# A decoder trunk on one core: the last pair of products reordered and stored in halves, the first weights loaded in blocks of two features

## The chip, the cores and the metric

The kernel runs on one core of a Trainium2 chip. The metric is the device time of one execution in microseconds; the number given for a kernel is the median of several runs.

A core has five engines that run at the same time and wait for one another through semaphores: TensorE (PE, matrix products; its weight loads are shown as PEld), VectorE (DVE), ScalarE (ACT), GpSimd (POOL) and SyncE (SP), which here only issues transfers. ScalarE and GpSimd can issue transfers too. Matrix products are written to PSUM, eight banks of 128 x 512 numbers; everything else lies in SBUF.

## What is computed

Two layers of a transformer trunk over 512 tokens of width 1024, in float32. Each layer has four parts, each added to the running sum x:

```python
x = x + 0.5 * swiglu(rms_norm(x, ffn1_norm[l]), ffn1_w_gate[l], ffn1_w_up[l], ffn1_w_down[l])
h = rms_norm(x, mix_norm[l])
a, g, q, k, v = split(h @ w_in[l])
# conv_out: a * sigmoid(g), causal depthwise convolution of width 31, rms_norm, silu
# diff_out: differential attention of q, k, v with a relative-position bias
x = x + concat([conv_out, diff_out]) @ w_out[l]
x = x + 0.5 * swiglu(rms_norm(x, ffn2_norm[l]), ffn2_w_gate[l], ffn2_w_up[l], ffn2_w_down[l])
# swiglu(h, g, u, d) = (silu(h @ g) * (h @ u)) @ d, inner width 2816
```

The result is x after the second layer.

## The kernel before, in words

**Layout.** x lies in SBUF with its width over the partitions: `x[:, k, :]`, k = 0 to 7, is one tile of 128 features by 512 tokens. Below, "feature k" means that tile of 128 features.

**Products in three parts.** A float32 operand is split into a high part (`whi` for weights, `acth` for activations), made by a copy on ScalarE, and the rest (`wlo`, `actl`), made by a subtraction on VectorE. One product then is three matmuls (`mm3`, lines 200, 203 and 204): high x high, high weight x low activation, low weight x high activation. Weights come from HBM into a ring of five buffers `wraw`, and their parts go to rings of nine buffers each.

**The start.** A few products of a tile of ones (`WARM`, line 228) run before any data is there. Then the first four weight tiles, gate and up for two output tiles, are loaded as two halves of four features each (`half`), and each half in blocks of columns that `cuts` gives: one feature and three features for the first half, all four at once for the second. For each block SP issues the first feature of x in it (line 238), the four weight blocks (line 241), and the rest of the features (line 247). Each weight block is converted on its own (lines 242, 243). `Prep.tile` makes `acth` and `actl` of each feature (lines 309, 310). `lead_products` multiplies all eight features with the four tiles, feature by feature; then the row sums of squares (`ssum`, lines 318 to 322) are transposed on TensorE (line 268).

`started` holds the last conversion on ScalarE and on VectorE of one block. The squares of x (on ScalarE) and the small scalars of `make_scalars` (on VectorE) are put behind it in their engines' order with `behind`. Before, that block is the last one of the first half.

**The order of the work.** A planner orders each engine's instructions, by a timeline that it simulates while the kernel is built; what is ready first in that timeline can go ahead of what stands earlier in the program. Calls of `keep_in_program_order` pin the first matmul of a group to its place among the pinned ones, and `behind` puts an engine's instructions after a given one. Waits between engines follow from the data.

**The feed-forward parts.** They use seven products of half-sized blocks in place of eight (Strassen's scheme in Winograd's form). The weight sums that it needs are made by loads that add on arrival (`wsum`, issued by GpSimd, line 160) and on VectorE (lines 175, 176). For the down projection a `Pair` computes two output tiles, m and m2 = m + 4, in two PSUM banks, each cut in two halves of 256 tokens: `a`, `d` in the first, `b`, `c` in the second. Each call of `go` (line 524) is one of the seven products; here it takes four steps of three matmuls, twelve in all. In the last pair (m = 3) the order on TensorE is: `c` (`t1`, in `head`, saved to `keep` at line 531), `d` (`t4`), the last product of the pair before, `a` (`b11`, after which both halves of the bank are saved, line 557), `b` (`b21`), `c` (`b22`), `a` (`t2`, saved at line 561), and in `finish` `a` (`t3`). `a` is a running sum: each product adds to it, so a save must have read it before the next product changes it.

Tile m = 3 is finished on VectorE by lines 563 and 564, once `c` holds everything. Tile 7 is finished in `finish`: line 570 adds a saved part to `d`'s place, line 571 another to `a`, and line 572 adds -0.5 times both to x. Then `store` (line 1070) writes the tile to HBM; each of the eight tiles is stored as soon as it is done, in one transfer on SP's queue. The function `tail` calls `finish` and the last `store`.

Of the kernel before, what the change touches and what calls it, by code (L numbers as in the profile page):

```python
# [15 lines left out]
ALU = mybir.AluOpType  # L16
# [6 lines left out]
KT = DM // P  # L23
# [14 lines left out]
MASK = -1e30  # L38
RLEN = 640
STATS_AT = 5  # L40
WARM = 9
TAIL_AT = 2
HS = SEQ // 2

# [26 lines left out]
def trunk(ctx: ExitStack, tc: tile.TileContext, xt, par, lamv, relb, onehot,  # L71
          gu1, dn1, wag, wqkv, wout, gu2, dn2, out):
    nc = tc.nc
    V, S, G, T = nc.vector, nc.scalar, nc.gpsimd, nc.tensor
# [9 lines left out]
    def f32(ap):  # L84
        return ap.bitcast(F32)
# [3 lines left out]
    def bank(tag, name):  # L89
        return psum.tile([P, 512], F32, tag=tag, name=name, bufs=BANKS[tag])  # L90
# [4 lines left out]
    def ring(tag, n=512):  # L95
        dt = F32R if tag in ("whi", "wlo") else F32
        return wp.tile([P, 512], dt, tag=tag, name=tag, bufs=RING[tag])[:, :n]
# [109 lines left out]
    x = act.tile([P, KT, SEQ], F32, tag="x", name="x")  # L207
# [17 lines left out]
    warm = bank("tp", "ps_warm")  # L225
    for _ in range(WARM):
        tc.keep_in_program_order(
# [1 line left out]
        )  # L229

    lead = [[] for _ in range(4)]
    for half, cuts in enumerate(((0, 1, 4), (0, 4))):
        tiles = [(ring("wraw"), ring("whi"), ring("wlo")) for _ in lead]
        for w, (_, hi, lo) in zip(lead, tiles):
            w.append((hi, lo))
        for k, k2 in zip(cuts, cuts[1:]):
            to = slice(k * P, k2 * P)
            nc.sync.dma_start(x[:, half * 4 + k, :], xt[half * 4 + k])
            for n, (raw, hi, lo) in enumerate(tiles):
                src = slice((half * 4 + k) * P, (half * 4 + k2) * P)  # L240
                nc.sync.dma_start(raw[:, to], gu1[0, n // 2, n % 2][:, src])
                big = S.activation(hi[:, to], raw[:, to], AF.Copy)
                low = V.tensor_tensor(out=lo[:, to], in0=raw[:, to], in1=f32(hi[:, to]), op=ALU.subtract)
            if k2 == 4 and not half:
                started = big, low
            for j in range(half * 4 + k + 1, half * 4 + k2):
                nc.sync.dma_start(x[:, j, :], xt[j])
    lead = [lead[2 * m : 2 * m + 2] for m in range(2)]
# [122 lines left out]
    def pair_banks():  # L371
        tag = ("sc", "po", "mm")[next(turns) % 3]
        return [bank(tag, "ps_pair") for _ in range(2)]
# [131 lines left out]
    class Pair:  # L505
# [10 lines left out]
        def go(self, ps, weight, xt, js=None):  # L516
            at = self.hid.get(xt)
            side = 0 if ps is self.a or ps is self.d else 1
            wh, wl = weight
            for i, j in enumerate(range(self.hid.n) if js is None else js):  # L520
                f = slice(j * P, (j + 1) * P)
                xh, xl = at(j)
                for l, (s, r) in enumerate(((wh, xh), (wh, xl), (wl, xh))):
                    mm = T.matmul(ps, s[:, f], r, start=side not in self.begun, stop=False, skip_group_check=True)  # L524
                    self.begun.add(side)
                    if i == l == 0:
                        tc.keep_in_program_order(mm)
# [3 lines left out]
            self.saved = S.activation(self.keep[:, self.kc], self.c, AF.Copy)  # L531
            return self

        def body(self, w, before, more=None):
            a, b, c, d, go = self.a, self.b, self.c, self.d, self.go
            both = self.banks[0].rearrange("p (n c) -> p n c", n=2)
            if self.m == 0:
                n = self.hid.n
                most, rest = range(n - 1), range(n - 1, n)
                go(a, w["g1"], "b11")  # L540
                more(S.activation(self.keep[:, 0], a, AF.Copy))
                go(b, w["g2"], "b21", most)
                go(d, w["u2"], "t4", most)
                nxt = before()
                go(c, w["all"], "b22", most)
                go(a, w["g1u2u1"], "t2", most)
                go(b, w["g2"], "b21", rest)
                go(c, w["all"], "b22", rest)
                go(d, w["u2"], "t4", rest)
                go(a, w["g1u2u1"], "t2", rest)  # L550
                saves.append(S.activation(self.keep[:, 2:], both, AF.Copy))
            else:
                nxt = None
                go(d, w["u2"], "t4")
                before()
                go(a, w["g1"], "b11")
                S.activation(self.keep[:, :2], both, AF.Copy)
                go(b, w["g2"], "b21")
                go(c, w["all"], "b22")
                go(a, w["g1u2u1"], "t2")  # L560
                saves.append(S.activation(self.keep[:, 2], a, AF.Copy))
            two, xm = self.banks[1].rearrange("p (n c) -> p n c", n=2), x[:, self.m, :]
            V.tensor_tensor(two, two, self.keep[:, 0::2], op=ALU.add)
            V.scalar_tensor_tensor(xm, self.banks[1], 0.5, xm, op0=ALU.mult, op1=ALU.add)
            return nxt

        def finish(self, weight):
# [3 lines left out]
            V.tensor_tensor(a, a, self.keep[:, self.kd], op=ALU.add)  # L571
            V.scalar_tensor_tensor(xn, self.banks[0], -0.5, xn, op0=ALU.mult, op1=ALU.add)

    def begin(pr, loads, tail=None):
        ws = [[chunk(src) for src in pair] for pair in loads]
        ps = [pair_banks() for _ in loads]
        return [*zip(ws, ps)], first_products(pr, ws, ps, early=tail is not None, tail=tail)

    def ffn(fp, pr, gu, dn, after, begun, then, spare, aside=None):
        halves = None  # L580
        late = []
        jobs = []
# [29 lines left out]
        for fs, kind in PARTS:  # L612
            many = len(fs)
            hh, held = [], []
            if kind == "first":
                for mm, m in enumerate(fs):
# [7 lines left out]
                    else:  # L624
                        w, ps = [chunk(gu[m, 0]), chunk(gu[m, 1])], pair_banks()
# [16 lines left out]
                    if m == 1:  # L642
                        halves = Halves(fp, pr, r)
# [5 lines left out]
                w = banks = None  # L649
                for m in range(KT):  # L650
# [3 lines left out]
                    for kk in range(many):  # L654
                        b = m * many + kk
                        if b % 4 == 0:
                            w = [gather(dn, blocks[b : b + 4])]
# [11 lines left out]
            this = group(part=True)  # L669
            finish()  # L670
            pair = None
            for m in range(KT // 2):
                m2 = m + KT // 2
                if m == 0:

                    def more(saved):
                        with behind(saved, hid.last[0]):
                            this.split("all", "g1u2u1", "g1u1")

                    with behind(hid.big, hid.sum):  # L680
                        ahead[0].split("u2u1")
                    pair = Pair(hid, fp, m, m2).head(this.w["u2u1"])
                    nxt = pair.body(this.w, lambda: Pair(hid, fp, 1, 1 + KT // 2).head(ahead[0].w["u2u1"]), more)
                else:
                    this = group(after=hid.last if m == 1 else ())
                    pair = nxt if m == 1 else Pair(hid, fp, m, m2).head(this.w["u2u1"])
                    pair.body(this.w, finish)
                if kind == "last":
                    if m:
                        after(m2 - 1)  # L690
                    after(m)
                late.append(lambda pair=pair, this=this: pair.finish(this.w["g1u1"]))

        def tail():
            finish()
            after(KT - 1)

# [347 lines left out]
    pr = Prep(0, "ffn1_norm")  # L1045
# [12 lines left out]
    begun = [*zip(lead, banks)], lead_products(pr, lead, banks)  # L1058
    for l in range(DEPTH):
        nxt = {}  # L1060

        def preparing(gain, l2=l):
            def after(m):
                if m == 0:
                    nxt["p"] = Prep(l2, gain)
                nxt["p"].tile(m)
            return after

        def store(m):
            nc.sync.dma_start(out[m], x[:, m, :])  # L1070

        with tc.tile_pool(name="ffn", bufs=1) as fp:
            begun = ffn(fp, pr, gu1[l], dn1[l], preparing("mix_norm"), begun,
                        lambda tail: begin(nxt["p"], [[wag[l, c, i] for i in range(2)] for c in range(2)], tail),
                        (l == 0, 1), aside if l == 0 else None)
        mixer(l, nxt["p"], preparing("ffn2_norm"), begun)
        with tc.tile_pool(name="ffn", bufs=1) as fp:
            begun = begin(nxt["p"], [[gu2[l, m, i] for i in range(2)] for m in range(2)])
            if l + 1 < DEPTH:
                begun = ffn(fp, nxt["p"], gu2[l], dn2[l], preparing("ffn1_norm", l + 1), begun,  # L1080
                            lambda tail: begin(nxt["p"], [[gu1[l + 1, m, i] for i in range(2)] for m in range(2)], tail), (0, 1))
            else:
                ffn(fp, nxt["p"], gu2[l], dn2[l], store, begun, lambda tail: tail(), (0, 0))
        pr = nxt["p"]


# [72 lines left out]
```

## Time and profile before

| what | value |
|---|---|
| median of 3 runs | 1771.87 us (1771.71 to 1772.9) |
| the profiled execution | 1772.54 us |
| its span, first to last instruction | 1770.8 us |
| TensorE busy | 1759.9 us, 11853 matmuls |
| VectorE busy | 1470.9 us |
| ScalarE busy | 1039.5 us |
| GpSimd busy | 515.1 us |
| transferred | 257.79 MB |

The profile shows one execution. Times are counted from the span's start. A row of a group or of the order of time names the source line, the engine, the operation and the tiles as output<-inputs; what stands in square brackets behind a row is the engine's idle time before it, and what ended that. Matmuls are pipelined: the next starts before the one before has ended, so their lengths overlap, and idle time appears only where the gap is longer than that overlap. A row "x4" merges four neighbours, with the time from the first start to the last end. Rows marked SPq or ACTq are the issues of transfers; the time to landing runs from the issue until the data has arrived. The chain of waits follows the work that ended last backwards, from each instruction to what released it.

### The profile page before, as it was taken

What the parts mean: (1) busy time and instruction counts of PE and PEld (TensorE: products, weight loads), DVE (VectorE), ACT (ScalarE), POOL (GpSimd) and SP (SyncE); (2) the same over time, 40 slices, a digit from 0 to 9 for tenths busy, and PEclk for the clock granted to TensorE, in tenths of its full rate; (3) what the DMA queues carried; (4) which work ended last, traced back from release to release, by engine and by line L of the source; (5) the groups of instructions that cost most, each with busy time, mean ns of one, the idle gap of its engine ahead of it and who ended that gap; (6) DMA issues with size and microseconds to landing.
All of it is one profiled execution on the core that took longest, in us unless ns stands there. A gap on an engine that the chain in (4) does not pass through costs nothing.

```text
span 1770.8 us, 32986 instructions
## 1 busy us (share of the span) xinstructions
PE 1759.9 (99%) x11853; PEld 1621.3 (92%) x11853; DVE 1470.9 (83%) x2642; ACT 1039.5 (59%) x1951; POOL 515.1 (29%) x497
## 2 busy tenths in 40 slices
PE   9999999999999999999999999999999999999998
PEld 7799999988788899999988999999887888999998
DVE  7969888969877969889987798899698678698987
ACT  6546566755865436566644565666559554465664
POOL 1011112169970011112200121121798600111122
PEclk9999999999999999999999999999999999999999
DMA  7457677533223457687544577766231335577774
GB/s 222 135 135 184 166 197 190 135 122 96 71 78 113 123 130 178 172 198 177 143 144 108 149 176 180 194 161 177 81 113 48 101 105 134 133 184 173 194 176 126
DMA packets 165894, 257.79 MB, mean 146 GB/s; under 512 B 19191, under 2 KB 61958, under 8 KB 165728
## 3 DMA queue, kind: packets, MB, share of 16 engines
q1 hardware_dynamic: 129024, 201.38, 36.7%
q0 software_dynamic: 36416, 54.12, 19.0%
q8 instruction: 93, 1.52, 0.3%
q14 instruction: 73, 0.60, 0.1%
q10 hardware_dynamic: 288, 0.16, 0.0%
HBM read 253.48 MB, written 3.42 MB: 145 GB/s over the span
## 4 chain that ended last, share of the span: by engine, by line
PE 95%; DVE 2%; DMA 1%; POOL 1%; ACT 1%; issue 0%; SPq 0%; ACTq 0%; DVEq 0%; POOLq 0%
PE ps_pair L435 36%; PE ps_pair L524 17%; PE ps_pair L203 9%; PE ps_pair L204 9%; PE ps_pair L200 9%; PE ps_out L200 2%; PE ps_out L203 2%; PE ps_out L204 2%; PE ps_pair L815 2%; PE ps_pair L814 2%; PE ps_pair L813 2%; PE ps_sc L930 1%; PE ps_v L844 1%; PE ps_v L843 1%; PE ps_v L845 1%; POOL wlo L102 0%
## 5 line engine op out<-in xcount | busy, mean ns | idle before, releaser
L101 ACT ACTIVATE whi<-wraw 128x512 fp32r<-128x512 f32 x744 | 454.0, 628 | 421.9 <-PE ps_pair L203 174.8
L102 DVE TENSOR_TENSOR wlo<-wraw,whi 128x512 fp32r<-128x512 f32 x640 | 427.0, 685 | 116.7 <-ACT whi L101 105.2
L160 POOL DMA_DIRECT2D wsum<-in_gu x128 | 112.2, 907 | 703.7 <-DMA wsum<-in_gu 276.0
L435 PE MATMUL ps_pair<-acth,wlo 128*128 128x256 f32 x1024 | 289.8, 283 | 0.0
L435 PE MATMUL ps_pair<-actl,whi 128*128 128x256 f32 x1024 | 289.8, 283 | 0.0
L435 PE MATMUL ps_pair<-acth,whi 128*128 128x256 f32 x1024 | 289.8, 283 | 0.0
L435 PE MATMUL ps_pair<-th,whi 128*128 128x256 f32 x768 | 217.3, 283 | 0.0
L435 PE MATMUL ps_pair<-tl,whi 128*128 128x256 f32 x768 | 217.3, 283 | 0.0
L435 PE MATMUL ps_pair<-th,wlo 128*128 128x256 f32 x768 | 217.3, 283 | 0.0
L200 PE MATMUL ps_pair<-acth,whi 128*128 128x512 f32 x512 | 199.4, 394 | 0.5 <-ACT acth L309 0.4
L203 PE MATMUL ps_pair<-actl,whi 128*128 128x512 f32 x512 | 199.5, 390 | 0.3 <-DVE actl L310 0.3
L204 PE MATMUL ps_pair<-acth,wlo 128*128 128x512 f32 x512 | 199.2, 390 | 0.0
L435 PEld LDWEIGHTS ps_pair<-actl,whi 128*128 128x128 f32 x1024 | 196.6, 192 | 0.2
L435 PEld LDWEIGHTS ps_pair<-acth,whi 128*128 128x128 f32 x1024 | 196.6, 192 | 0.2
L435 PEld LDWEIGHTS ps_pair<-acth,wlo 128*128 128x128 f32 x1024 | 196.6, 192 | 0.0
L160 POOL DMA_DIRECT2D wsum<-in_dn x112 | 98.8, 1132 | 266.6 <-DMA wsum<-in_dn 45.6
L435 PEld LDWEIGHTS ps_pair<-th,whi 128*128 128x128 f32 x768 | 147.5, 192 | 0.0
L435 PEld LDWEIGHTS ps_pair<-tl,whi 128*128 128x128 f32 x768 | 147.5, 192 | 0.0
L435 PEld LDWEIGHTS ps_pair<-th,wlo 128*128 128x128 f32 x768 | 147.5, 192 | 0.0
L102 POOL TENSOR_TENSOR wlo<-wraw,whi 128x512 fp32r<-128x512 f32 x104 | 137.1, 1339 | 31.8 <-ACT whi L101 19.5
L524 PE MATMUL ps_pair<-hh,whi 128*128 128x256 f32 x512 | 144.9, 283 | 0.0
L524 PE MATMUL ps_pair<-hl,whi 128*128 128x256 f32 x512 | 144.9, 283 | 0.0
(207 smaller groups left out, 4445.2 us busy)
## 6 DMA issues: line engine op xcount, KB each, us to landing
wraw<-in_gu SPq DMA_DIRECT2D x284, 256.0 KB, 3.5
wsum<-in_gu SPq DMA_DIRECT2D x128, 256.0 KB, 3.8
wsum<-in_gu POOLq DMA_DIRECT2D x128, 256.0 KB, 4.7
wraw<-in_dn SPq DMA_DIRECT2D x68, 256.0 KB, 3.3
wraw<-in_wqkv SPq DMA_DIRECT2D x48, 256.0 KB, 2.9
wraw<-in_wout SPq DMA_DIRECT2D x48, 256.0 KB, 3.0
wraw<-in_dn SPq DMA_DIRECT2D x64, 128.0 KB, 4.2
wraw<-in_wag SPq DMA_DIRECT2D x32, 256.0 KB, 3.0
```

What stands on the lines that cost most here:

```text
L101: S.activation(hi, raw, AF.Copy)
L102: (eng or V).tensor_tensor(out=lo, in0=raw, in1=f32(hi), op=ALU.subtract)
L160: nc.gpsimd.dma_start(dst[:, to], src, accum_op=ALU.add)
L200: first = T.matmul(ps, wh, xh, start=start, stop=False)
L203: T.matmul(ps, wh, xl, start=False, stop=False)
L204: T.matmul(ps, wl, xh, start=False, stop=stop)
L435: mm = T.matmul(ps, l, r, start=first and i == j == 0, stop=False, skip_group_check=True)
L524: mm = T.matmul(ps, s[:, f], r, start=side not in self.begun, stop=False, skip_group_check=True)
L813: T.matmul(ps[n], xh[:, t], wh, start=k == 0, stop=False)
L814: T.matmul(ps[n], xh[:, t], wl, start=False, stop=False)
L815: T.matmul(ps[n], xl[:, t], wh, start=False, stop=k == KT - 1)
L843: T.matmul(ps, xh[:, t], wh, start=k == 0, stop=False)
```

## The change

Four edits.

- The products of ones (`WARM`) go from nine to eight.
- The first weights come in blocks of two features throughout: `cuts` becomes (0, 2, 4) for both halves. There are sixteen weight transfers of 128 KB in place of four of 64, four of 192 and four of 256 KB. x's features 0, 2, 4 and 6 go ahead of their block, and 1, 3, 5 and 7 behind it. `started` is set by every block, so it ends up as the last block of the second half.
- In the last pair of the last feed-forward part, `b22` (into `c`) comes after `t2` and its save in place of before them.
- The last tile of the output, tile 7, is finished in another way there: -0.5 times the two saved parts is added to x by one operation on 512 columns, ahead of the product `t3`; after `t3`, -0.5 times `a` is added to each half of 256 tokens, and each half is stored by a transfer of its own, the first issued on SP and the second on ScalarE's queue.

```diff
-WARM = 9
+WARM = 8
...
-    for half, cuts in enumerate(((0, 1, 4), (0, 4))):
+    for half, cuts in enumerate(((0, 2, 4), (0, 2, 4))):
...
-            if k2 == 4 and not half:
-                started = big, low
+            started = big, low
...
-        def body(self, w, before, more=None):
+        def body(self, w, before, more=None, last=False):
...
                 go(b, w["g2"], "b21")
-                go(c, w["all"], "b22")
+                if not last:
+                    go(c, w["all"], "b22")
                 go(a, w["g1u2u1"], "t2")
                 saves.append(S.activation(self.keep[:, 2], a, AF.Copy))
+                if last:
+                    go(c, w["all"], "b22")
...
+        def finish_halves(self, weight, store):
+            a, xs = self.a, x[:, self.m2, :].rearrange("p (n c) -> p n c", n=2)
+            V.scalar_tensor_tensor(xs, self.keep[:, 1::2], -0.5, xs, op0=ALU.mult, op1=ALU.add)
+            self.go(a, weight, "t3")
+            for n, queue in enumerate((nc.sync, nc.scalar)):
+                V.scalar_tensor_tensor(xs[:, n], a, -0.5, xs[:, n], op0=ALU.mult, op1=ALU.add)
+                store(n, xs[:, n], queue)
...
-                    pair.body(this.w, finish)
+                    pair.body(this.w, finish, last=kind == "last" and end and m == KT // 2 - 1)
...
-        def tail():
+        def tail(halves=None):
+            if halves:
+                late.clear()
+                pair.finish_halves(this.w["g1u1"], halves)
+                return
             finish()
             after(KT - 1)
...
+        def store_half(n, half, queue):
+            queue.dma_start(out[KT - 1][:, n * HS : (n + 1) * HS], half)
...
-                ffn(fp, nxt["p"], gu2[l], dn2[l], store, begun, lambda tail: tail(), (0, 0))
+                ffn(fp, nxt["p"], gu2[l], dn2[l], store, begun, lambda tail: tail(store_half), (0, 0), end=True)
```

More of the change, by code (lines that the diff above doesn't have):

```diff
@@ L577, in begin, with ffn @@
         return [*zip(ws, ps)], first_products(pr, ws, ps, early=tail is not None, tail=tail)
-    def ffn(fp, pr, gu, dn, after, begun, then, spare, aside=None):
+    def ffn(fp, pr, gu, dn, after, begun, then, spare, aside=None, end=False):
         halves = None
```

## The prediction

> **What bounds the kernel now.** I read the page first (busy time by engine), then TensorE's waits, then the matmuls at both ends in order of time, because the change touches nothing else.
>
> ```profile
> PE 1759.9 (99%) x11853; PEld 1621.3 (92%) x11853; DVE 1470.9 (83%) x2642; ACT 1039.5 (59%) x1951; POOL 515.1 (29%) x497
> ```
> ```profile
> PE ps_pair L524 <- ACT keep L557: 0.9, 2, 0.5
> ...
> PE ps_pair L524 <- ACT keep L561: 0.5, 1, 0.5
> ```
> ```profile
> 30.00:1700.00 1670.00, 1667.37 (x11209) 1535.42 (x11208) 1395.04 (x2498) 984.91 (x1848) 497.66 (x471) 1.00 0.56 144
> ```
>
> TensorE is busy for 1759.9 of 1770.8 us, so the change can win only what TensorE loses: some 11 us in all. In the 1670 us between the ends it loses 2.6 (the row of a stage: its length, then TensorE's busy time), so what is to be had lies in the first 30 us and behind the last products, where the diff works: one wait there is that on the save of line 561. Matmuls are pipelined, so the waits shown are too small; the loss is read from start to start.
>
> TensorE's first products in order of time (start, length, line, out<-in, count):
>
> ```profile
> 1.44 4.21 PE L228 MATMUL ps_warm<-ones_r 128*128 128x512 f32 x9 [1.44 <-DVE ones_r L221]
> 5.44 0.81 PE L200 MATMUL ps_pair<-acth,whi 128*128 128x512 f32 x2
> 6.10 0.63 PE L203 MATMUL ps_pair<-actl,whi 128*128 128x512 f32 x2
> ...
> 8.63 0.39 PE L203 MATMUL ps_pair<-actl,whi 128*128 128x512 f32 x1
> 9.09 0.50 PE L200 MATMUL ps_pair<-acth,whi 128*128 128x512 f32 x1
> ...
> 11.07 0.61 PE L204 MATMUL ps_pair<-acth,wlo 128*128 128x512 f32 x2
> 12.10 1.20 PE L200 MATMUL ps_pair<-acth,whi 128*128 128x512 f32 x4 [0.42 <-ACT acth L309]
> 13.58 0.50 PE L203 MATMUL ps_pair<-actl,whi 128*128 128x512 f32 x1 [0.28 <-DVE actl L310]
> ...
> 15.53 1.07 PE L200 MATMUL ps_pair<-acth,whi 128*128 128x512 f32 x4
> ...
> 29.13 0.60 PE L268 MATMUL ps_rows<-ident,ssum 128*128 128x128 f32 x4
> ```
>
> Undisturbed, four products take 1.07 us, so one follows another after (1.07 - 0.39)/3 = 0.227. The first products are 8 features x 4 tiles x 3 = 96, or 21.8 us; from 5.44 to 29.13 they take 23.7. Of the 1.9 too many, 0.2 is the first one still at half pace; the rest is three stalls, after 8.63, 11.07 and 12.10, some 1.6 with the slow restart behind each.
>
> **The change part by part: the start.** What stalled them is in ScalarE's and VectorE's rows; SP's issues, their time to landing and a piece of the chain of waits follow:
>
> ```profile
> 10.30 0.61 ACT L318 ACTIVATE ssum<-x 128x512 f32<-128x512 f32 x1
> 10.82 0.61 ACT L321 ACTIVATE sq<-x 128x512 f32<-128x512 f32 x1
> 11.35 0.71 ACT L309 ACTIVATE acth<-x,par 128x512 fp32r<-128x512 f32 x1
> ...
> 11.88 0.68 DVE L322 TENSOR_TENSOR ssum<-ssum,sq 128x512 f32<-128x512 f32 x1
> ...
> 12.78 0.75 DVE L310 SCALAR_TENSOR_TENSOR actl<-x,par,acth 128x512 fp32r<-128x512 f32 x1
> ```
> ```profile
> 3.05 0.43 SPq L238 DMA_DIRECT2D x<-in_xt  x1
> ...
> 5.70 0.90 SPq L247 DMA_DIRECT2D x<-in_xt  x2
> ...
> x<-in_xt SPq DMA_DIRECT2D x1, 256.0 KB, 3.2
> ...
> x<-in_xt SPq DMA_DIRECT2D x1, 256.0 KB, 4.8
> ...
> 5.22 4.62 DMA wraw<-in_gu
> ```
>
> Feature 2 of x, issued at 5.70, landed 4.8 later, at 10.5; ScalarE then did two squares before its `acth` at 11.35, and VectorE a sum of squares and small scalars before its `actl` at 12.78. With `started` set by the last conversion of the last block, squares and scalars queue behind all sixteen conversions and can't come before feature 2. That removes the second and third stall (0.81 - 0.23 = 0.58 and 0.67 - 0.23 = 0.45 between starts, 0.11 each for the restart). The first (0.46 - 0.23 = 0.23, and 0.11) waited for the three-feature blocks; with two features in the first block, feature 1 needs no second load.
>
> Whether loads keep up I count in bytes on SP's queue ahead of each piece (par's 159 KB included; a tile of x is 256 KB, a block of two features 128). Before, x1 landed at 3.05 + 3.2 = 6.25 after 927 KB, the last three-feature block at 9.84 after 1695, x2 at 10.5 after 1951. After, x1 is complete at 1183 KB: 6.25 + 256/768 x 3.59 = 7.4, its `acth` 0.71 later at 8.2, and TensorE ends feature 0 at 8.3. The second blocks end at 1951 KB, at 10.5, 10.9 with a conversion of some 0.4; TensorE wants feature 2 at 11.0. So it fits, by a hair: I take 1.5 of the 1.6, and 0 to 1.6 as ends. The four issues more (at 0.43) delay the next group's loads on SP from 12.3 to some 13.9; these wait for buffers and are wanted at 27, so nothing. The squares move on ScalarE from 10.3 to about 18: eight at 0.61 and their sums end by 25, where the transposes of the row sums would start at 27.4. Cover stays.
>
> One product of ones fewer: 4.21 us hold nine, so one is about 0.43. But the first real product needs its converted weights:
>
> ```profile
> 4.54 1.00 ACT L242 ACTIVATE whi<-wraw 128x128 fp32r<-128x128 f32 x4
> ...
> 5.02 0.76 PEld L200 LDWEIGHTS ps_pair<-acth,whi 128*128 128x128 f32 x2
> ...
> 1756.33 0.36 ACT L531 ACTIVATE keep<-ps_pair 128x256 f32<-128x256 f32 x1
> ```
>
> The first 128-column conversion starts at 4.54; one of 256 columns takes 0.36, so the weight load starts at 4.9 to 4.95 in place of 5.02: 0.1 gained (ends 0 and 0.43). Start: 1.6 in all. It reaches the end, since TensorE has almost no idle time until then and its weights wait for buffers that it frees itself.
>
> **The end.**
>
> ```profile
> 1759.26 0.60 ACT L557 ACTIVATE keep<-ps_pair 128x512 f32<-128x512 f32 x1 [2.57 <-PE ps_pair L524]
> ...
> 1763.26 0.28 PE L524 MATMUL ps_pair<-yh,wlo 128*128 128x256 f32 x1
> 1763.58 0.38 ACT L561 ACTIVATE keep<-ps_pair 128x256 f32<-128x256 f32 x1 [3.72 <-PE ps_pair L524]
> 1763.99 0.70 DVE L563 TENSOR_TENSOR ps_pair<-ps_pair,keep 128x512 f32<-128x512 f32 x1 [4.54 <-ACT keep L561]
> 1764.01 0.38 PE L524 MATMUL ps_pair<-yh,whi 128*128 128x256 f32 x1 [0.47 <-ACT keep L561]
> 1764.72 0.69 DVE L564 SCALAR_TENSOR_TENSOR x<-ps_pair,x 128x512 f32<-128x512 f32 x1
> ...
> 1765.42 0.28 PE L524 MATMUL ps_pair<-yh,wlo 128*128 128x256 f32 x1
> 1765.73 0.43 DVE L570 TENSOR_TENSOR ps_pair<-ps_pair,keep 128x256 f32<-128x256 f32 x1 [0.32 <-PE ps_pair L524]
> 1766.67 0.69 DVE L572 SCALAR_TENSOR_TENSOR x<-ps_pair,x 128x512 f32<-128x512 f32 x1
> ```
> ```profile
> 1765.44 2.28 SPq L1070 DMA_DIRECT2D out<-x  x2
> ...
> GB/s 0 0 0 0 0 0 0 0 137 382 423 396 341 69 0 0 0 0 0 0 0 164 369 410 396 355 55 55 0 0 0 0 0 0 0 0 0 0 0 0
> ...
> out<-x SPq DMA_DIRECT2D x2, 256.0 KB, 2.1
> ```
>
> Today the twelve `t2` products end at 1763.54, ScalarE saves them, and only then may the twelve `t3` products overwrite: the last starts at 1765.42. With the `b22` products between, the save (0.38) lies under 12 x 0.12 = 1.44 us of products, `t3` follows without a gap, and its last starts at 1763.26 + 1.44 = 1764.70, 0.72 earlier, ending at 1764.98. VectorE now starts line 563 at about 1763.57 and line 564 at 1764.30, through at 1764.99. The new product of `keep` with -0.5 (512 columns, 0.69) needs saves that exist at 1759.9, or 1762.5 if the strided read is held to wait for the save of `t2`; VectorE is idle there for 4.54 us, so I price it at nothing (0.6 if it is ordered behind line 564). The halves take 0.43 each in place of 0.43 + 0.43 + 0.69: the first from 1765.01 to 1765.44, the second, overlapping, to 1765.79, where line 572 ended at 1767.36.
>
> Stores: tile 3's issue moves from 1765.44 to 1765.03; the halves are issued at about 1765.47 on SP and 1765.82 on ScalarE's idle queue. In the GB/s row (0.15 us a slice, from 1765) 256 KB begin 0.85 after the issue and flow for 0.85; landing comes at 2.1. Three stores together are 512 KB, from 1765.88 to 1767.6, and land at 1768.0; today the last is issued at 1767.39 and lands at 1769.49. Gain 1.5. Were the queues to have separate engines, the last half would land about 1.65 after its issue, at 1767.5 (gain 2.0); with the 0.6 above, 0.9. I take 1.5, nearest to the rate of the row, which is near 400 GB/s for a store alone.
> The Trainium skill ("DMA: Bandwidth & Descriptors", Issuing engines are not separate DMA queues) says that issuing from several engines saves the sequencer's time only. By that rule the sum keeps 1.5; without it 2.0. No run yet shows two store queues at once.
>
> **Sum.** 1772.54 (the profiled execution; its span is 1770.8) - 1.6 - 1.5 = 1769.4. The median of the three runs, 1771.87, lies 0.67 lower, so 1768.8.
>
> **The rivals.** (1) More than the sum: a stall elsewhere goes with the shift (line 557 has 0.9) or the second half finds free engines (0.5) or the weights are ready for the whole 0.43: about 0.9 more, 1767.9. For it: thin waits; against: nothing in the diff aims there.
> (2) The start brings nothing: the larger blocks come late and each feature waits again. For it: margins of 0.1 above; against: the early loads, 64 KB per 0.43 us of issue, leave the engines room, and the squares are gone in any case. 1768.8 + 1.6 = 1770.4.
> (3) TensorE's clock rises later. The products of ones start (4.21 - 0.63) / 8 = 0.45 apart and the first two real ones 0.42, from 6.10 on it is 0.23: full pace came 4.5 us after the first start at 1.44. If the gap of some 0.1 before the real products makes that count begin anew at 5.35, it comes at 9.85; about 3.95 us at half pace lose half, 2.0: 1770.8. Against it: the gap is shorter than a product.
> The Trainium skill ("TensorE: Matmul & The Clock Gate", Part 1) says that the gate looks at free-running windows of about 3.4 us of activity and doesn't count products. By it eight products or nine matter only through that gap, and one window later would cost 1.7, an estimate from the page's figure. The trace shows one rise and not where a window begins, so it bears out neither.
> (4) Slower than before. The order of ScalarE, VectorE, SP and POOL is written by a planner from its own clock, which the start shifts; one accumulating weight load moved behind others in its queue is late by a transfer. In the chain one takes this long:
>
> ```profile
> 1742.83 6.04 DMA wsum<-in_dn
> ```
>
> TensorE lost 0.5 on line 557 just behind that transfer, so there is no slack there and another 6.0 would come whole: 1768.8 + 6.0 = 1774.8. It decides from 3.1 us on. Against it: the 2.6 us lost between the ends so far, and an order that follows from buffers which TensorE frees.
>
> **How the numbers follow.** What a measurement of this kernel can tell from no change is about 0.2%, 3.5 us: below 1768.3 is faster, above 1775.4 slower. Forecast 0.55 (a third of it below 1768.3, own range 1767.8 to 1769.8); (1) 0.18; (2) and (3) 0.15; (4) 0.12, two thirds of it above 1775.4. Faster 0.18 + 0.18 = 0.36, slower 0.08, same 0.56. The range runs from the best ends of the start (2.0) and of the end (2.0) with 0.7 of the waits between, 1768.8 - 0.4 - 0.5 - 0.7 = 1767.2, to rival (3) with the 0.6 of the end lost as well and 0.2 over, 1771.6.
>
> **What would show it.** Starts of the first 96 products: 22 us from first to the transposes, none over 0.3 apart, squares after 17 us. At the end no gap before `t3`, line 563 beginning with it, two 256-column products on `out`'s last tile, last landing about 3.1 us earlier. Wrong if the stalls return at features 1 to 3, if products run at half pace past 6.5 us, if `keep` x -0.5 stands behind line 564, or if a new wait appears between 30 and 1750 us.

## The result, and the profile after

The median fell from 1772.16 to 1768.97 us (22 runs of each), 3.2 us; the ratio is 0.9984, with a 95% interval of 0.9977 to 0.999, or 1.8 to 4.1 us less. The forecast was 1768.8.

The profiled execution is not a typical one: at 1772.28 us it is the slowest of the 22. TensorE's waits in it and two pieces of the chain of waits say why:

```profile
PE ps_pair L523 <- ACT keep L556: 2.3, 2, 2.1
PE ps_pair L523 <- ACT keep L530: 1.6, 1, 1.6
```
```profile
1093.55 6.10 DMA wsum<-in_gu
```
```profile
1742.31 8.22 DMA wsum<-in_dn
```

ScalarE converts weights and saves parts in one queue. Where a weight load that adds on arrival is late, the save behind its conversion is late (lines 530 and 556 after are 531 and 557 before), and TensorE waits. The piece at 1742 took 6.04 before and 8.22 here. The same kernel in another execution (1769.81 us, span 1768.0; all its waits of TensorE) lost next to nothing there:

```profile
PE ps_warm L228 <- DVE ones_r L221: 1.4, 1, 1.4
PE ps_o L974 <- ACT at L967: 1.1, 2, 0.5
PE ps_sc L944 <- DVE e L958: 0.8, 2, 0.4
PE ps_pair L523 <- ACT keep L556: 0.4, 2, 0.2
PE ps_pair L200 <- DVE gs L642: 0.3, 1, 0.3
```

Neither list has the old waits on `acth`, `actl` and on the save of line 561; a wait on `gs` (line 642) is new. By stages, from the starts of TensorE's matmuls in the order of time (us):

| | before | after, first profile | after, second profile |
|---|---|---|---|
| first real product | 5.44 | 5.02 | 5.02 |
| clock at full pace from | 5.8 | 5.0 | 7.4 |
| first product of the first seven-product stage | 107.97 | 106.43 | 107.42 |
| first product of the last four pairs' run | 1723.79 | 1723.81 | 1723.20 |
| last product of all | 1765.42 | 1766.36 | 1763.87 |
| from there to the end of the span | 5.35 | 4.14 | 4.15 |

The start after, first profile, in the order of time:

```profile
1.44 3.74 PE L228 MATMUL ps_warm<-ones_r 128*128 128x512 f32 x8 [1.44 <-DVE ones_r L221]
5.02 0.40 PE L200 MATMUL ps_pair<-acth,whi 128*128 128x512 f32 x1
5.35 0.50 PE L203 MATMUL ps_pair<-actl,whi 128*128 128x512 f32 x1
...
7.99 1.07 PE L200 MATMUL ps_pair<-acth,whi 128*128 128x512 f32 x4
...
10.71 0.62 PE L200 MATMUL ps_pair<-acth,whi 128*128 128x512 f32 x2
...
28.39 0.60 PE L267 MATMUL ps_rows<-ident,ssum 128*128 128x128 f32 x4
...
38.67 0.40 PE L204 MATMUL ps_pair<-acth,wlo 128*128 128x512 f32 x1
39.32 0.50 PE L200 MATMUL ps_pair<-acth,whi 128*128 128x512 f32 x1 [0.25 <-DVE gs L642]
```

The first real product follows the last product of ones with no gap, and from 5.35 to 38.67 no stall stands between two products. (The row sums' transposes come at 28.39, not 27.4, because the planner put six products of the third tile ahead of them.) At 39.32 TensorE is held up: 0.65 from start to start in place of 0.23.

The end, second profile: ScalarE's save and TensorE around `t3`'s first product (1762.55), VectorE's operations, SP's and ScalarE's issues, the stores' time to landing:

```profile
1761.31 0.38 ACT L561 ACTIVATE keep<-ps_pair 128x256 f32<-128x256 f32 x1 [2.28 <-PE ps_pair L523]
```
```profile
1762.43 0.28 PE L523 MATMUL ps_pair<-hh,wlo 128*128 128x256 f32 x1
1762.55 0.28 PE L523 MATMUL ps_pair<-yh,whi 128*128 128x256 f32 x1
```
```profile
1762.83 0.70 DVE L565 TENSOR_TENSOR ps_pair<-ps_pair,keep 128x512 f32<-128x512 f32 x1 [3.07 <-PE ps_pair L523]
1763.56 0.69 DVE L566 SCALAR_TENSOR_TENSOR x<-ps_pair,x 128x512 f32<-128x512 f32 x1
1764.19 0.76 DVE L581 SCALAR_TENSOR_TENSOR x<-ps_pair,x 128x256 f32<-128x256 f32 x2
```
```profile
1764.28 0.33 SPq L1084 DMA_DIRECT2D out<-x  x1
1764.72 0.37 SPq L1087 DMA_DIRECT2D out<-x  x1
```
```profile
1764.98 0.35 ACTq L1087 DMA_DIRECT2D out<-x  x1
```
```profile
out<-x SPq DMA_DIRECT2D x1, 256.0 KB, 2.0
out<-x SPq DMA_DIRECT2D x1, 128.0 KB, 2.0
out<-x ACTq DMA_DIRECT2D x1, 128.0 KB, 2.1
```

The save now lies under products, `t3` goes on at the usual 0.12, and the second half is issued 1.10 us after the last product's start, where the whole tile was issued 1.97 after it before. The halves are 128 KB and land as long after their issue, 2.0 to 2.1, as 256 KB do.

### The profile page after: what moved, and what is told of

The parts are those of the page before. It is cut to its first block, busy times and chain, and to the rows that moved or that the text cites. A ratio compares the mean times of both kernels' runs of the same rounds, so it can differ in the third digit from the quotient of the medians.

```text
span 1770.5 us, 33000 instructions
## 1 busy us (share of the span) xinstructions
PE 1758.8 (99%) x11852; PEld 1620.9 (92%) x11852; DVE 1470.9 (83%) x2646; ACT 1037.4 (59%) x1955; POOL 516.1 (29%) x497
## 4 chain that ended last, share of the span: by engine, by line
PE 94%; DVE 2%; DMA 1%; POOL 1%; ACT 1%; issue 1%; DVEq 0%; ACTq 0%; SPq 0%; POOLq 0%
PE ps_pair L434 36%; PE ps_pair L523 16%; PE ps_pair L200 9%; PE ps_pair L203 9%; PE ps_pair L204 9%; PE ps_out L200 2%; PE ps_out L203 2%; PE ps_out L204 2%; PE ps_pair L829 2%; PE ps_pair L828 2%; PE ps_pair L827 2%; PE ps_sc L944 1%; PE ps_v L858 1%; PE ps_v L859 1%; PE ps_v L857 1%
## 5 line engine op out<-in xcount | busy, mean ns | idle before, releaser
L102 DVE TENSOR_TENSOR wlo<-wsum,whi 128x512 fp32r<-128x512 f32 x192 | 130.0, 683 | 23.7 <-ACT whi L101 23.4
```

Source lines behind the costliest of these rows:

```text
L102: (eng or V).tensor_tensor(out=lo, in0=raw, in1=f32(hi), op=ALU.subtract)
```

## The experiments

Each kernel was timed beside the kernel before on the same chip; "before" is its median there.

**The two ends apart.** Only the three edits of the start, and only those of the end:

```diff
 start_only, against the kernel before
-WARM = 9
+WARM = 8
-    for half, cuts in enumerate(((0, 1, 4), (0, 4))):
+    for half, cuts in enumerate(((0, 2, 4), (0, 2, 4))):
-            if k2 == 4 and not half:
-                started = big, low
+            started = big, low
 end_only, against the changed kernel: these lines as before
```

> The three edits of the start alone (eight products of ones, blocks of two features, squares behind the last block), the end as before. Theory (two separate gains that TensorE carries to the end): 1.6 us below the kernel before, read in the trace as the first matmul of the seven-product stage starting at 106.4 in place of 108.0 us, and no two of the first 96 products over 0.35 us apart once the clock is up; the end from the last product on takes as long as before (5.35 us from the last start of a matmul to the end of the span). Rival (start brings nothing that lasts, all is won at the end): same time as before, first seven-product matmul at 108.0 or later stages that take it back.

> The edits of the last pair and of the last store alone, the start as before. Theory: 1.5 us below the kernel before by the prediction's sum; the two profiles so far give 0.7 us between the last pair's first product and its last, and 1.2 us from there to the end of the span, 1.8 together. First seven-product matmul at 108.0 as before. Rival (the end gains only the removed wait, 0.7 us, since three stores crowd on the same engines): 0.7 below the kernel before.

Measured: start 1771.24 against 1772.62 before (0.9992, 0.9984 to 1.0001), end 1770.97 (0.9994, 0.9986 to 1.0003): 1.4 and 1.7 us, 3.0 together, about the whole change. Each interval alone just reaches 1, but the traces show each gain at its place. With the start alone the first seven-product matmul stands at 106.61 (before 107.97); with the end alone the last product's start comes 40.75 us after that of the last run of pairs (before 41.63), and the rest takes 4.72 us (before 5.35). So both gains arise, each without the other, and the rival of the end falls.

Whether the start's gain lasts to the end is less clear. In the profile with the start alone the last run of pairs begins at 1723.52, only 0.27 before the 1723.79 of before: of the lead of 1.36 TensorE lost 1.0 near 1100 us, on the save of line 530. The three profiles with the old start (before, `end_only` and `swap_only` below) have the first seven-product matmul at 107.76 in the mean and the last run of pairs at 1723.55; the five with all edits of the start and eight products of ones (both of the changed kernel, `start_only`, and `halves_sp` and `whole_store` below) have them at 106.84 and 1723.63. The lead is 0.9 in the mean and then gone: four of the five lost 1.0 to 1.6 near 1100 us. But these five executions were 1.1 us longer in the mean than their kernels' medians, and the three 0.6 shorter. That the gain lasts in a typical execution rests on the medians: 1.4 here, and 2.6 for the blocks alone below, whose interval excludes no change.

One expectation failed: with the start alone the time behind the last product fell too, from 5.35 to 5.01, although no instruction of it changed. After the last landing SP runs down a list of waits on semaphores at 0.06 each. From the one that waits for that landing on, seven are left before, three with the start alone, six with the end alone and two in the changed kernel. Of the 0.34 here, 0.24 is that list; the store itself landed 0.09 earlier.

**How many products of ones.**

```diff
-WARM = 8
+WARM = 9    (ones_nine, against the changed kernel)
+WARM = 5    (ones_five)
```

> The changed kernel with nine products of ones in place of eight. Theory (the first product waits for its weights, so the ninth product costs little): 0.1 us above the changed kernel, first real product at 5.4 us. Rival (the weights are there, the whole product of ones is on the path): 0.4 us above it. If the clock's rise depends on the count of products, it comes at the same place in both.

> The changed kernel with five products of ones in place of eight, so that TensorE is idle for about 1 us before the first real product. Theory of the prediction's third rival (an idle gap makes the clock's count begin anew): full pace comes 4.5 us after the first real product, at about 9.4 us, and the kernel is 2.0 us slower than the changed one. Rival (the gate looks at windows whose place does not depend on the kernel, and a gap of 1 us in a window may or may not count): full pace between 5 and 9 us, differing from one execution to the next, 0 to 1.7 us slower.

Measured: nine 1769.25, five 1771.38, beside 1772.62 before. Nine starts its first real product at 5.44, where eight start it at 5.02 without a gap: the weights are ready early enough, and the ninth product is wholly on the path (the rival, 0.4); in time it is 0.3 above the changed kernel's 22 runs, within noise. Five, in the order of time on TensorE:

```profile
2.46 1.48 PE L228 MATMUL ps_warm<-ones_r 128*128 128x512 f32 x3
4.94 0.80 PE L200 MATMUL ps_pair<-acth,whi 128*128 128x512 f32 x1 [1.00 <-ACT whi L242]
...
7.33 0.63 PE L200 MATMUL ps_pair<-acth,whi 128*128 128x512 f32 x1
7.75 0.63 PE L203 MATMUL ps_pair<-actl,whi 128*128 128x512 f32 x1
...
10.31 1.41 PE L200 MATMUL ps_pair<-acth,whi 128*128 128x512 f32 x4
11.56 0.39 PE L203 MATMUL ps_pair<-actl,whi 128*128 128x512 f32 x1
11.79 0.39 PE L204 MATMUL ps_pair<-acth,wlo 128*128 128x512 f32 x1
```

One microsecond of idle time, and products start 0.43 apart, half pace, until about 11.0, 6.1 us after the first real one. The kernel is 2.1 us slower than with nine, near the 2.0 of the count that begins anew; but that theory put the rise at 9.4, and it came 1.6 later. The Trainium skill ("TensorE: Matmul & The Clock Gate", Part 1) has free-running windows of some 3.4 us. With eight or nine products full pace came between 4.4 and 7.4 us in the thirteen profiles of before, after and the other experiments, a spread of 3.0, narrower than one such window, and with five at 11.0, 3.6 behind the latest of them. The traces' own rows of the granted clock agree with the page: the stretch at full clock lasts 1764.69 us in seven of the thirteen, 1761.28 in the other six and 1757.86 with five, in steps of 3.41. How much idle time in a window delays the rise stays open. One profile of the five doesn't exclude another rule: in the thirteen the rise came 3.0 to 6.0 us after TensorE's first product, and with five 6.1 us after the first product behind the gap, so a count that begins anew there would nearly fit too.

**Blocks against squares.** The kernel before with the new `cuts` alone, and with the new place of `started` alone:

```diff
 blocks_only
-    for half, cuts in enumerate(((0, 1, 4), (0, 4))):
+    for half, cuts in enumerate(((0, 2, 4), (0, 2, 4))):
 squares_late
-            if k2 == 4 and not half:
-                started = big, low
+            started = big, low
```

> The kernel before with blocks of two features alone: nine products of ones, and squares and scalars still queued behind the first half's last block. Theory A (each edit removes its own stall, as the prediction had it): only the stall that waited for the three-feature blocks goes, 0.3 us, and squares and scalars still hold up a feature: first seven-product matmul 0.3 us earlier than before. Theory B (the squares now stand ahead of feature 4, which TensorE wants only at 16 us): all stalls of the start go, 1.6 us.

> The kernel before with squares and scalars queued behind the last block of the second half alone, blocks of one, three and four features as before. Theory A: the second and third stall go and the first stays, 1.25 us. Rival: the loads of x's features 2 and 3, behind the three-feature blocks, are what was late (x2 landed at 10.5), so no more than 0.5 us.

Measured: the blocks 1770.46, the squares 1773.49, beside 1773.03 before; ratios 0.9987 (0.9977 to 0.9996) and 1.0003 (0.9994 to 1.0013). TensorE's waits in the first 60 us, of the squares alone first, then of the blocks alone:

```profile
PE ps_warm L228 <- DVE ones_r L221: 1.4, 1, 1.4
PE ps_pair L200 <- ACT whi L242: 0.4, 1, 0.4
PE ps_pair L200 <- DVE gs L631: 0.3, 1, 0.3
```
```profile
PE ps_warm L228 <- DVE ones_r L221: 1.4, 1, 1.4
```

Theory B holds: with blocks alone no wait is left in the list, squares in their old place and all. From start to start two products at half pace stand 0.58 and 0.59 apart in place of 0.43, 0.3 in all. The first seven-product matmul stands at 107.06, 0.9 earlier than before and not the 1.6 of theory B; full pace came only at 7.2 in this execution, 1.4 later than before, which costs up to half of that. Moving the squares alone does remove the second and third stall, as theory A says, but the first stays and is larger (the wait on line 242; products at 9.04 and 9.80), and a wait on `gs` comes up near 40 us. The first seven-product matmul stands at 107.98, as before: of the 1.25 us of theory A nothing came.

That wait on `gs` is in all eight profiles with late squares and in none of the six with early ones. With late squares the row sums end later (27.8 us in the changed kernel's first profile, 25.3 before), and the planner puts five to eight products of the third tile ahead of the transposes that read them. So VectorE clears the first tile's banks later, and after 144 products, three tiles of 48, the fourth tile's products need a bank.

**The end, part by part.** The kernel before with the order alone:

```diff
 swap_only
-                go(c, w["all"], "b22")
+                if not last:
+                    go(c, w["all"], "b22")
                 go(a, w["g1u2u1"], "t2")
                 saves.append(S.activation(self.keep[:, 2], a, AF.Copy))
+                if last:
+                    go(c, w["all"], "b22")
```

> The kernel before with the last pair's products reordered alone; tile 7 is finished by the three old operations and stored whole. Theory: the gap before the last twelve products goes (0.6 to 0.7 us) and all after the last product takes as long as before, 5.0 to 5.35 us: 0.7 us in all. Rival (VectorE's two operations for tile 3, which now begin later relative to the products, get in the way of tile 7's): 0.3 us or less.

Measured: 1773.21 against 1773.03 (0.9999, 0.999 to 1.0008): the time shows nothing, and the interval holds 0.7 as well. In the trace the gap is gone, the wait on line 561 with it, and 5.38 us follow the last product's start, as before. The four profiles with the old order have 0.75 and then 0.22 between products there, the ten with the new one 0.12 each: 0.73 us. So the mechanism is seen in the trace; its worth in time, alone, stays open.

The changed kernel with both halves on SP's queue, and with one operation and one store:

```diff
 halves_sp
-            for n, queue in enumerate((nc.sync, nc.scalar)):
+            for n, queue in enumerate((nc.sync, nc.sync)):
 whole_store
-            for n, queue in enumerate((nc.sync, nc.scalar)):
-                V.scalar_tensor_tensor(xs[:, n], a, -0.5, xs[:, n], op0=ALU.mult, op1=ALU.add)
-                store(n, xs[:, n], queue)
+            V.scalar_tensor_tensor(
+                xs, a.unsqueeze(1).broadcast_to([P, 2, HS]), -0.5, xs, op0=ALU.mult, op1=ALU.add
+            )
+            store(x[:, self.m2, :])
```

> The changed kernel with both halves of the last tile issued on SP's queue. Theory (all queues feed the same engines, a queue of its own saves the issue alone): the second half is issued 0.15 us later, behind the first one's issue, and lands 0.1 to 0.2 us later than in the changed kernel. Rival (a second queue brings engines or bandwidth of its own): 0.5 us later.

> The changed kernel with tile 7 finished by one operation on 512 columns after the last product and stored whole by SP; the operation on the saved parts ahead of the last product stays. Theory (the gain behind the last product is that of the two operations moved ahead, not of the halves): the operation takes 0.69 us, is issued at 1.04 us after the last product's start in place of 1.10, and lands about 3.1 us after it, as the halves do (3.2): same time as the changed kernel within 0.1 us. Rival (the halves overlap operation and store): lands 0.4 to 0.5 us later.

Measured: on SP 1770.8 (1773.03 before, 0.9988, 0.9978 to 0.9997); whole 1769.45 (1773.21 before, 0.9977, 0.9968 to 0.9986). From SP the second half is issued at 1.31 after the last product's start in place of 1.10, and lands at 3.17, as from ScalarE: 0.2 later out and no later in. So a queue of its own gives nothing that one profile of each shows; with the end alone the same half, from ScalarE, landed at 3.50, so a landing can vary by 0.3. The whole tile lands at 3.09. Its one operation and the two stores (the other one is tile 3):

```profile
1764.33 0.69 DVE L566 SCALAR_TENSOR_TENSOR x<-ps_pair,x 128x512 f32<-128x512 f32 x1
1764.96 0.69 DVE L580 SCALAR_TENSOR_TENSOR x<-ps_pair,x 128x512 f32<-128x512 f32 x1
```
```profile
out<-x SPq DMA_DIRECT2D x2, 256.0 KB, 2.0
```

One operation of 0.69 is over before the two halves (0.76 together), and its store lands as fast. What wins behind the last product is that two of three operations no longer stand there; the halves add nothing.

**The changed kernel again, and with early squares.** The second differs from it by

```diff
 squares_early
-            started = big, low
+            if k2 == 4 and not half:
+                started = big, low
```

> The changed kernel once more, beside the next two on the same chip, to have its profile in an execution without late accumulating loads. Theory (the two long waits of its first profile, behind line 530 near 1100 us and line 556 near 1751 us, are loads that were late in that execution, not an order of the planner's): at least one of them is shorter by 1 us or absent here, and the kernel is again 3.0 to 3.3 us below the kernel before. Rival (the new order makes them): both are there again with 1.5 us and more.

> The changed kernel with squares and scalars queued behind the first half's last block, as in the kernel before. Theory (moving them back is what makes TensorE wait for VectorE at the third gate-and-up group near 39 us, 0.4 us and 0.1 of restart, and the blocks alone took away the stalls of the start): no such wait, first 96 products still without a stall, 0.5 us below the changed kernel. Rival (squares ahead of a feature stall the products again): 0.3 to 1.2 us above it.

Measured, beside 1773.21 before: again 1769.98 (0.9984, 0.9975 to 0.9993), early squares 1769.06 (0.9979, 0.997 to 0.9988). The second profile of the changed kernel, shown above, lacks the wait near 1100 us and has 0.4 behind line 556 in place of 2.3: late loads, not an order, and the rival falls. The load is the one that the chain names: issued near 1093 us, it landed after 6.1 to 6.9 us in the four profiles with a wait of 1.0 to 1.6 behind line 530, and after 3.7 to 5.2 in the ten others. All four are among the seven profiles with both late squares and the new blocks; that the new start makes such a late load more likely is not excluded. The instructions of VectorE, ScalarE, GpSimd and SP also stand in the same sequence before and after from 78 us on until the last pair. With early squares TensorE's waits in the first 60 us are the one on the tile of ones, and VectorE begins to clear the first bank 1.3 us earlier (first row: the changed kernel's first profile; last row: early squares; between them, its waits):

```profile
38.58 0.69 DVE L642 TENSOR_TENSOR gs<-ps_pair,rb 128x512 f32<-128x512 f32 x1
```

```profile
PE ps_warm L228 <- DVE ones_r L221: 1.4, 1, 1.4
```
```profile
37.31 0.69 DVE L643 TENSOR_TENSOR gs<-ps_pair,rb 128x512 f32<-128x512 f32 x1
```

That is 0.9 lower than the changed kernel on the same chip, with overlapping intervals; the trace accounts for 0.5.

**Both findings together.** `early_whole` has the edits of `squares_early` and `whole_store`.

> The changed kernel with both findings put in: squares and scalars behind the first half's last block, and tile 7 finished by one operation and stored whole. Theory (the two are independent): no wait near 39 us, last landing 3.1 us after the last product's start, 3.5 to 4.0 us below the kernel before, which is about 0.5 below the changed kernel. Rival (the planner's order of the rest shifts again): a new wait of TensorE between 40 and 1750 us that the other kernels don't show.

Measured: 1768.55 against 1773.3 (0.9975, 0.9966 to 0.9984), 4.7 us below the kernel before, more than the 3.5 to 4.0 expected, and the lowest ratio of all; the changed kernel had 0.9984, and the intervals overlap. No new wait; the last landing comes at 3.1:

```profile
PE ps_warm L228 <- DVE ones_r L221: 1.4, 1, 1.4
PE ps_o L976 <- ACT at L969: 1.1, 2, 0.5
PE ps_sc L946 <- DVE e L960: 0.8, 2, 0.4
PE ps_pair L524 <- ACT keep L531: 0.2, 1, 0.2
```

## Why the prediction was right, and where its steps were not

**The sum** said 3.1 less, 1768.8; it became 3.2 less, 1768.97. The two ends were forecast at 1.6 and 1.5 and measured alone at 1.4 and 1.7. With an interval of 1.8 to 4.1 for the whole, a hit within 0.2 is in part luck. That the start's gain reaches the end, since TensorE is the bound, held for the medians; four of the five profiles lost it again, mostly to the load near 1093 us.

**The three stalls of the start.** That they disappear held. Their size (1.6) is that of one execution: `swap_only`, with the same start, has 1.6 as well, but `end_only`, where full pace came at 6.8, has two stalls and 0.9. The cause was given wrongly: the prediction let the late squares remove the second and third. The blocks remove all three, and squares need not move.

**"Cover stays".** This step failed. Late squares were priced at nothing because their sums would end by 25, ahead of the transposes at 27.4. The last sums on VectorE, before and after (first profile):

```profile
24.59 0.68 DVE L322 TENSOR_TENSOR ssum<-ssum,sq 128x512 f32<-128x512 f32 x1
```
```profile
25.54 2.28 DVE L321 TENSOR_TENSOR ssum<-ssum,sq 128x512 f32<-128x512 f32 x3
```

They ended at 27.8, and the 96 products were through at 27.0. The planner filled that time with the six products of the third tile, so TensorE lost nothing at the transposes. But all that follows from the row sums came later too, and it ends in clearing the banks of the first tile: at 38.58, 1.3 later than with early squares. There was no such slack, and TensorE lost 0.42 there with 0.1 for the restart.

**One product of ones fewer.** Mis-sized: 0.1 was taken and 0.42 came (5.44 to 5.02), the upper end. The weight load came when it was forecast, at 4.9 (first profile after):

```profile
4.87 0.24 PEld L200 LDWEIGHTS ps_pair<-acth,whi 128*128 128x128 f32 x1 [0.37 <-ACT whi L242]
```

But the product follows it by 0.15 here, where before it stood 0.42 behind a load at 5.02: it had waited for the ninth product of ones, not for its weights. This error and the one before nearly cancel, and the start came out right by that luck.

**The end.** The order of the products held: the gap went, worth 0.73 where 0.72 was forecast. (The 0.88 between 41.63 and 40.75 holds 0.15 more, from a shorter wait near 1751 us in that execution.) The operation on `keep`, priced at nothing, ran in VectorE's idle time long before line 565 (columns as above, first profile after):

```profile
1761.55 0.69 DVE L578 SCALAR_TENSOR_TENSOR x<-keep,x 128x512 f32<-128x512 f32 x1 [0.45 <-ACT keep L556]
1765.31 0.70 DVE L565 TENSOR_TENSOR ps_pair<-ps_pair,keep 128x512 f32<-128x512 f32 x1 [3.07 <-PE ps_pair L523]
```

The last half was put at an issue 1.12 and a landing 3.3 after the last product's start and has 1.10 and 3.17, where the whole tile landed at 4.07 before. That the engines are shared held (`halves_sp`). The 0.3 from the final list of waits was not foreseen, and it helps the sum. The halves as such, which the working counted as part of the gain, are worth nothing.

**The rivals.** (1) No stall elsewhere goes with the shift, but single parts were larger than forecast. (2) did not occur. (3) did not occur with eight, as no gap arose; with five full pace came late, by another rule than the one priced. (4): the order did not change from 78 us on, yet late loads cost up to 2.1 us at one place, in single executions of the same kernel. Two of the prediction's signs of being wrong did appear: half pace past 6.5 us (7.4 in the second profile; but 7.2 and 7.3 with nine products too, so it isn't the change that makes it) and a new wait between 30 and 1750 us, the one on `gs`. The second is the step that failed.

## What to carry to other kernels

Where one engine is busy for 99% of the time, a change is worth what it takes from that engine's gaps, and those are read from start to start at the place of the edit; here that gave a sum within the measured interval. A lead won early can be lost to a later wait in a single execution, so compare it at several places and in more than one profile. When work is moved out of one stage's way, follow its result to the last buffer that it frees: other products covered for the late row sums at their reader, and a PSUM bank further on was still late. At the end of a kernel, count the dependent operations between the last product and the store: taking two of three out of there won what there was, and cutting the store in halves won nothing.

## What was not expected of the hardware

- The moment at which products reach full pace moves between executions: 4.4 to 7.4 us after the start of the span, with the same or nearly the same start. Two profiles of the changed kernel differ by 1.0 us at the first seven-product matmul (106.43 and 107.42) with the rise at 5.0 and 7.4.
- A load that adds on arrival took 6.5 to 9.3 us from issue to landing at one and the same place near 1084 us in fourteen profiles; TensorE's wait behind the save near 1100 us lay between nothing and 1.6. The two don't go strictly together: one profile had 8.6 and no wait. With the load issued near 1093 us they do: 6.1 us and more with the wait, 5.2 and less without.
- 256 KB and 128 KB last stores land equally long after the issue (2.0 to 2.1 us in most profiles) when another store runs just ahead of them; single ones took 2.2 (256 KB) and 2.4 (128 KB).
- The end of this kernel has a list of waits at 0.06 us each, and their place before or behind the last landing is worth 0.3 us.
